# One series of 16x16 inverses on 128 partitions in place of two on 64, in a two-layer hybrid decoder step

## The chip, the cores and the metric

The kernel runs on one core of a Trainium2 chip. The metric is the device time of one execution in microseconds (us). All times in the text are of one profiled execution, in us from the start of its span, unless a sentence says otherwise. Engines: PE is TensorE (matmuls; PEld its weight loads), DVE is VectorE, ACT is ScalarE, POOL is GpSimd, and SP is SyncE, whose queue issues nearly all DMAs here.

## The reference, cut to what matters

One inference step of a decoder with two layers, on a prompt of 512 tokens and on 8 sequences of 4 sample tokens, model width 1024. A layer is a norm, one input projection (`w_in`) whose columns feed four mixers, an output projection (`w_out`), and an MLP (`w_up`, squared ReLU, `w_down`):

```python
h = rms_norm(x, prm['g_mix_pre'])
p_rw, p_s5, p_gdn, p_swa = split_cols(h @ prm['w_in'], PROJ_SPLITS)
o_rw, rw_shift, rw_S = rwkv7_mixer(p_rw, rw_shift, rw_S, prm)      # RWKV-7
o_s5, s5_re, s5_im = s5_mixer(p_s5, s5_re, s5_im, prm)             # S5
o_gdn, gdn_conv, gdn_S = gdn_mixer(p_gdn, gdn_conv, gdn_S, prm)    # gated delta rule
o_swa, swa_k, swa_v = swa_mixer(p_swa, swa_k, swa_v, start, prm['swa_sinks'])
mix = jnp.concatenate([o_rw, o_s5, o_gdn, o_swa], axis=-1) @ prm['w_out']
x = x + rms_norm(mix, prm['g_mix_post'])
f = jnp.square(jax.nn.relu(rms_norm(x, prm['g_mlp_pre']) @ prm['w_up'])) @ prm['w_down']
x = x + rms_norm(f, prm['g_mlp_post'])
```

The delta rule solves, for each chunk of 64 tokens and each head, a lower triangular system with ones on its diagonal (a 64x64 triangle A):

```python
U = lax.linalg.triangular_solve(eye + A, rhs, left_side=True, lower=True, unit_diagonal=True)
```

RWKV's recurrence, which the reference writes token by token, is computed by the kernel in chunks of 64 too, and needs the inverse of such a triangle as well.

## The kernel before

**Halves and mixers.** The tokens are worked in two halves of 256 prompt tokens; the second carries the 32 sample tokens too (288 columns). `body()` writes the work in this order: projection of half 0, mixers of half 0, `w_out` of half 0, mixers of half 1, MLP of half 0, `w_out` of half 1, and so on through the second layer; the projection of half 1 is written among the mixers of half 0. So there are four places where mixers run: place 1 (layer 0, half 0), place 2 (layer 0, half 1), place 3 (layer 1, half 0) and place 4 (layer 1, half 1).

**Order on the engines.** The program is put in order ahead of time by a scheduler that goes by priorities: `PRIO` gives a number to a named section (`gd2` 3000, `norm` 800, `rw2` 392, `rwt` 300, `gdt` 200, and so on; the section `rw3` and the matmuls of `dense` have none). Each engine, and SP's queue, then works through its own list strictly in the order written; an instruction that waits holds up all that stand behind it.

**Dense matmuls.** `dense` works unit by unit: 24 matmuls of 128x128 weights on 256 or 288 columns, in two half-units of 12. A half-unit is one 256 KB load into `wraw` (5 buffers), a cast on ACT into `whi` (3 buffers), a subtraction on DVE into `wlo` (3 buffers), and 12 matmuls (`ps<-h,whi` and `ps<-h,wlo`). The result banks of `dense` rotate over 3 buffers (bank "mm"), and the sliding-window mixer's rope, a matmul of a copied result with a permutation (`ps<-e,cst`), takes its bank from the same three. DVE frees that bank by `e<-ps,g`, which multiplies it by the rope table (a `g2` tile loaded by SP behind the delta rule's end, `last_gd`).

**The triangles.** `tri_begin` makes the inverses of the 16x16 blocks on the diagonals of a mixer's triangles: two DMAs write the triangles to DRAM (`trsc`), one gathers the diagonal blocks into a tile `c` of 64 partitions (64 blocks, one to a partition); then 23 DVE operations, each on the result of the one before (seven pairs of a product `c<-t,c` and a sum `t<-c` on 8x8 blocks, two rounds of four on the off-diagonal 8x8 blocks, one copy `t<-t`); two DMAs write the inverses and their transposes to a zeroed DRAM image (`diag`), and four read them back as block-diagonal 64x64 tiles (`t<-diag`: `t16t` and `t16`). `tri_end` then builds the whole inverses by matmuls (`ps<-t,t`) and DVE additions. `rw_stage2` (section `rw2`) and `gd_stage2` (section `gd2`) each call `tri_begin`; `gd_stage3` (`gdt`) and `rw_stage3` (`rwt`) call `tri_end`. All these tiles, and the RWKV triangles `lt` themselves, are of class `t2`, which has 5 buffers. What follows is `rw_chain` and `gd_chain` (a recurrence over four chunks), `rw_post` and `gd_post` (norm and gate; their results go to DRAM as `mix`), and `s5_main` (loads of its kernels `s5kin`, two small convolutions on PE, scans on DVE, products on POOL, 40 small matmuls for y, gelu, a round trip through DRAM `s5sz`, and a gate: the matmuls `ps<-r,r` 128x256 called GLU below). `w_out` of a half needs `mix` of all four mixers.

Of the kernel before, what the change touches and what calls it, by code (L numbers as in the profile page):

```python
# [139 lines left out]
class K:  # L140
# [133 lines left out]
    def tri_begin(self, lt, which):  # L274


        nc = self.nc
# [4 lines left out]
        for c in range(2):
            self.nc.sync.dma_start(out=rows(sc, c), in_=lt[64 * c:64 * c + 64])
        gp = self.w([64, 17, 16], "c1")
        g = gp[:, 0:16]
# [211 lines left out]
    def rw_stage2(self, l, r):  # L497
# [25 lines left out]
        tri = self.tri_begin(lt, 0)  # L523
# [26 lines left out]
        r.update(rp=rp, xv=xv, bk=bk, xw=xw, z=z, kt=kt, tri=tri)  # L550
# [330 lines left out]
    def gd_stage2(self, l, r):  # L881
# [11 lines left out]
        r.update(sco=sco, tri=self.tri_begin(sco[:, :, 1], 1))  # L893

    def gd_stage3(self, l, r):
# [22 lines left out]
        self.inv_apply(self.tri_end(*r["tri"]), kg, wt, lambda h, b, cs: vt[cs, h // 2, b, 64 * (h % 2):64 * (h % 2) + 64], xw)  # L918
# [1118 lines left out]
```

## Time and profile before

| what | value |
|---|---|
| three runs | 1645.79, 1649.16 and 1655.67 us; median 1649.16 |
| the profiled execution | 1651.66 us, its span 1649.9 us |
| PE busy / PEld busy | 1562.9 us (95%) / 1458.9 us (88%) |
| DVE busy | 1216.6 us (74%), 2959 instructions |
| ACT / POOL busy | 964.7 us (58%) / 312.8 us (19%) |
| granted TensorE clock, mean | 0.976 |

PE is busy nearly throughout, so the time is that of PE's work, plus the idle gaps in it, plus what stretches at the lower clock cost. A saving on another engine is worth what it takes out of PE's gaps. The gaps of PE over 0.5 us sum to 75.9 us; they lie at the start and end, and around the places where mixers and norms meet.

### The profile page before, as it was taken

What the parts mean: (1) busy time and instruction counts of PE and PEld (TensorE: products, weight loads), DVE (VectorE), ACT (ScalarE), POOL (GpSimd) and SP (SyncE); (2) the same over time, 40 slices, a digit from 0 to 9 for tenths busy, and PEclk for the clock granted to TensorE, in tenths of its full rate; (3) what the DMA queues carried; (4) which work ended last, traced back from release to release, by engine and by line L of the source; (5) the groups of instructions that cost most, each with busy time, mean ns of one, the idle gap of its engine ahead of it and who ended that gap; (6) DMA issues with size and microseconds to landing.
All of it is one profiled execution on the core that took longest, in us unless ns stands there. A gap on an engine that the chain in (4) does not pass through costs nothing. (4 is left out here: it accounts for less than half of the span.)

```text
span 1649.9 us, 38760 instructions
## 1 busy us (share of the span) xinstructions
PE 1562.9 (95%) x14472; PEld 1458.9 (88%) x14472; DVE 1216.6 (74%) x2959; ACT 964.7 (58%) x2094; POOL 312.8 (19%) x614
## 2 busy tenths in 40 slices
PE   6989999799999999799999999999999899999996
PEld 6878878689888999788899999989898899999996
DVE  6799785986696868778485667889668865866665
ACT  6676557654345468575465467886444456855544
POOL 4651241100112424600020002520002101100001
PEclk9999998999999999999999999999999999999998
DMA  6635443443356566435356556535534665655452
GB/s 216 197 111 129 150 148 122 118 114 122 125 192 228 191 207 231 135 96 149 117 191 190 166 160 205 184 110 147 137 119 146 226 216 188 204 193 165 161 168 104
DMA packets 205416, 267.37 MB, mean 162 GB/s; under 512 B 81114, under 2 KB 98844, under 8 KB 204812
## 3 DMA queue, kind: packets, MB, share of 16 engines
q1 hardware_dynamic: 203308, 258.73, 49.5%
q0 software_dynamic: 1920, 6.17, 1.0%
q8 instruction: 113, 1.85, 0.4%
q14 instruction: 75, 0.61, 0.1%
HBM read 237.95 MB, written 28.58 MB: 162 GB/s over the span
## 5 line engine op out<-in xcount | busy, mean ns | idle before, releaser
L232 ACT CAST whi<-wraw 128x512 fp32r<-128x512 f32 x752 | 462.8, 619 | 420.4 <-PE ps L220 244.7
L236 DVE TENSOR_TENSOR wlo<-wraw,whi 128x512 fp32r<-128x512 f32 x752 | 537.6, 721 | 215.1 <-ACT whi L232 187.2
L220 PE MATMUL ps<-h,whi 128*128 128x288 f32 (+1 forms) x3264 | 517.4, 298 | 12.7 <-ACT whi L232 6.0
L220 PEld LDWEIGHTS ps<-h,whi 128*128 128x128 f32 x3264 | 453.8, 193 | 29.3 <-ACT whi L232 7.7
L220 PE MATMUL ps<-f,whi 128*128 128x288 f32 (+1 forms) x2752 | 426.6, 294 | 5.9 <-ACT whi L232 2.8
L220 PEld LDWEIGHTS ps<-f,whi 128*128 128x128 f32 x2752 | 375.5, 191 | 17.3 <-ACT whi L232 4.3
L220 PE MATMUL ps<-h,wlo 128*128 128x288 f32 (+1 forms) x1632 | 291.9, 297 | 4.6 <-DVE wlo L236 4.3
L220 PEld LDWEIGHTS ps<-h,wlo 128*128 128x128 f32 x1632 | 238.0, 192 | 13.7 <-DVE wlo L236 7.6
L220 PE MATMUL ps<-f,wlo 128*128 128x288 f32 (+1 forms) x1376 | 236.2, 293 | 7.3 <-DVE wlo L236 7.2
L220 PEld LDWEIGHTS ps<-f,wlo 128*128 128x128 f32 x1376 | 197.3, 191 | 11.9 <-DVE wlo L236 8.7
L236 POOL TENSOR_TENSOR sums<-sums,d 128x288 f32<-128x288 f32 (+1 forms) x60 | 61.1, 1019 | 537.1 <-ACT d L228 532.9
L236 DVE TENSOR_TENSOR acc<-acc,ps 128x256 f32<-128x256 f32 (+1 forms) x96 | 41.7, 435 | 51.9 <-PE ps L220 51.7
L232 ACT CAST f<-d 128x288 fp32r<-128x288 f32 (+1 forms) x128 | 53.4, 417 | 35.7 <-DVE d L236 35.5
L220 PE MATMUL ps<-r,r 64*64 64x64 f32 (+7 forms) x1184 | 68.3, 237 | 6.3 <-DMA r<-s5m 3.1
L220 PEld LDWEIGHTS ps<-r,r 64*64 64x64 f32 (+4 forms) x1184 | 56.6, 140 | 15.5 <-issue 8.0
L228 ACT ACTIVATE d<-ps 128x256 f32<-128x256 f32 (+1 forms) x156 | 61.4, 394 | 13.3 <-PE ps L220 11.4
L228 ACT ACT_TABLE_LOAD x45 | 57.7, 1283 | 0.8
L236 DVE TENSOR_TENSOR f<-d,f 128x288 fp32r<-128x288 f32 (+1 forms) x128 | 55.4, 434 | 1.9 <-ACT f L232 1.7
L236 DVE TENSOR_TENSOR d<-d 128x288 f32<-128x288 f32 (+1 forms) x128 | 55.7, 435 | 0.3 <-ACT d L228 0.3
L232 ACT COPY e<-ps 128x256 f32<-128x256 f32 (+2 forms) x96 | 28.0, 325 | 18.1 <-PE ps L220 8.5
L220 PE MATMUL ps<-t,t 64*64 64x64 f32 x1024 | 36.5, 221 | 2.0 <-DMA t<-diag 2.0
L220 PEld LDWEIGHTS ps<-t,t 64*64 64x64 f32 x1024 | 32.6, 135 | 6.2 <-DMA t<-diag 2.4
(393 smaller groups left out, 1846.9 us busy)
## 6 DMA issues: line engine op xcount, KB each, us to landing
wraw<-in_w_up SPq DMA_DIRECT2D x256, 256.0 KB, 2.8
wraw<-in_w_down SPq DMA_DIRECT2D x256, 256.0 KB, 2.9
wraw<-in_w_in SPq DMA_DIRECT2D x176, 256.0 KB, 3.0
wraw<-in_w_out SPq DMA_DIRECT2D x64, 256.0 KB, 3.2
t<-diag SPq DMA_DIRECT2D x32, 128.0 KB, 3.2
x<-acc SPq DMA_DIRECT2D x3, 1152.0 KB, 5.3
x<-acc SPq DMA_DIRECT2D x3, 1024.0 KB, 5.1
xs<-mix SPq DMA_DIRECT2D x8, 288.0 KB, 3.3
```

Source lines behind the costliest of these rows:

```text
L220: return self.nc.tensor.matmul(out=out, lhsT=lhsT, rhs=rhs, start=start, stop=stop)
L228: return self.nc.scalar.activation(out=out, in_=in_, func=func, scale=scale, bias=bias, **kw)
L232: return self.nc.scalar.copy(out, in_)
L236: return (eng or self.nc.vector).tensor_tensor(out=out, in0=a, in1=b, op=op)
```

## The change

One `tri_begin` takes both triangles. Its tiles have 128 partitions, RWKV's 64 blocks on the lower half and the delta rule's on the upper; the 23 DVE operations and the two memsets on POOL are there once for both, after both gathers. It is called at the end of section `gd2`. The writes to `diag` are issued for the delta rule first (`for w in (1, 0)`). `t16t`, `t16` and `work` are now allocated in `tri_end`, which also issues the reads `t<-diag`. The number of DMAs stays. DVE has 92 instructions fewer (four series of 23), POOL eight.

```diff
-    def tri_begin(self, lt, which):
+    def tri_begin(self, lts):
...
-        for c in range(2):
-            self.nc.sync.dma_start(out=rows(sc, c), in_=lt[64 * c:64 * c + 64])
-        gp = self.w([64, 17, 16], "c1")
+        gp = self.w([128, 17, 16], "c1")
         g = gp[:, 0:16]
-        self.nc.sync.dma_start(out=g, in_=blocks(sc))
-        t16t, t16, work = (self.w([128, 8, 64], "t2") for _ in range(3))
...
+        half = lambda w: slice(64 * w, 64 * w + 64)
+        for w, lt in enumerate(lts):
+            sc = self.t([64 * 1040], "trsc", pool="dram", bufs=2)
+            for c in range(2):
+                self.nc.sync.dma_start(out=self.tri_rows(sc, c), in_=lt[64 * c:64 * c + 64])
+            self.nc.sync.dma_start(out=g[half(w)], in_=self.tri_blocks(sc))
+
+        tt2 = self.w([128, 2, 16, 16], "t2")
         tt = tt2[:, 0]
-        tmp = self.w([64, 16, 16], "c1")
+        tmp = self.w([128, 16, 16], "c1")
...
         nc.vector.tensor_copy(tt2[:, 1].rearrange("p j c -> p c j"), tt)
+        for w in (1, 0):
+            for x in range(2):
+                self.nc.sync.dma_start(out=self.tri_blocks(self.diag[w][x]), in_=tt2[half(w), x])
...
-        for x, t in enumerate((t16t, t16)):
-            d = self.diag[which][x]
-            self.nc.sync.dma_start(out=blocks(d), in_=tt2[:, x])
-            for c in range(2):
-                self.nc.sync.dma_start(out=t[64 * c:64 * c + 64], in_=rows(d, c))
-        return lt, t16, t16t, work
-
-    def tri_end(self, lt, t16, t16t, work):
+    def tri_end(self, lt, which):
+        t16t, t16 = (self.w([128, 8, 64], "t2") for _ in range(2))
+        for x, t in enumerate((t16t, t16)):
+            for c in range(2):
+                self.nc.sync.dma_start(out=t[64 * c:64 * c + 64], in_=self.tri_rows(self.diag[which][x], c))
+        work = self.w([128, 8, 64], "t2")
...
-        tri = self.tri_begin(lt, 0)
...
-        self.inv_apply(self.tri_end(*r["tri"]), r["kt"], r["wt"], r["z"], r["xw"])
+        self.inv_apply(self.tri_end(r["lt"], 0), r["kt"], r["wt"], r["z"], r["xw"])
...
-        r.update(sco=sco, tri=self.tri_begin(sco[:, :, 1], 1))
+        r.update(sco=sco, lt=sco[:, :, 1])
...
             self.gd_stage2(l, gd)
+            self.tri_begin((rw["lt"], gd["lt"]))
```

The scheduler gives other orders to the engines around it. Three places of place 1 are shown.

**SP, the reads of the inverses.** `diag00` and `diag01` are RWKV's, `diag10` and `diag11` the delta rule's, `wraw` the loads of half-units of `w_in`. Before:

```order
L1659 DMA wraw_547_2871<-in_w_in 128x512
L316 DMA diag00_270_1399<-t2_350_1694 64x16x16
L316 DMA diag01_271_1400<-t2_350_1694 64x16x16
L318 DMA t2_348_1692<-diag00_270_1399 64x8x64 x2
L318 DMA t2_349_1693<-diag01_271_1400 64x8x64 x2
L1659 DMA wraw_552_2903<-in_w_in 128x512
```

After, where the delta rule's inverses are read:

```order
L315 DMA diag10_272_1403<-t2_364_1784 64x16x16
L315 DMA diag00_270_1399<-t2_364_1784 64x16x16
L315 DMA diag11_273_1404<-t2_364_1784 64x16x16
L315 DMA diag01_271_1400<-t2_364_1784 64x16x16
L331 DMA t2_399_1944<-diag10_272_1403 64x8x64 x2
L331 DMA t2_400_1945<-diag11_273_1404 64x8x64 x2
```

and, 11 loads of `w_in` further on, where RWKV's are:

```order
L1670 DMA wraw_628_3354<-in_w_in 128x512
L331 DMA t2_411_2080<-diag00_270_1399 64x8x64 x2
L1670 DMA wraw_631_3372<-in_w_in 128x512
L1670 DMA wraw_636_3394<-in_w_in 128x512
L1670 DMA wraw_639_3412<-in_w_in 128x512
L331 DMA t2_412_2081<-diag01_271_1400 64x8x64 x2
```

Before, RWKV's inverses were read at once and ahead of the delta rule's (7 `w_in` loads ahead of their writes); after, they come behind the delta rule's by 11 loads for the first tile and 14 for the second. The load of the S5 kernels (`r4<-s5kin0`), which had ten `w_in` loads behind it in place 1, now stands behind the last of them.

**PE, at the 41st unit of `w_in` of half 1** (960 dense matmuls of that half done). `ps<-e1` is the rope's permutation, `ps<-r2,r4` S5's y, `ps<-g2,cst`, `ps<-r2,cst` and `ps<-acc,rwg2` belong to `gd_post` and `rw_post`, `ps441` to the end of RWKV's chain. Before:

```order
L220 MATMUL ps665_3547<-e1_664_3545,cst_6_77 128x288 [waits Activation_49]
L220 MATMUL ps666_3552<-h9_284_1440,whi_668_3554 128x288 x4
L220 MATMUL ps666_3552<-h9_285_1441,whi_668_3554 128x288 x4
L220 MATMUL ps666_3552<-h9_284_1440,wlo_669_3555 128x288 x4
L220 MATMUL ps666_3552<-h9_284_1440,whi_671_3572 128x288 x4
L220 MATMUL ps666_3552<-h9_285_1441,whi_671_3572 128x288 x3
L220 MATMUL ps478_2468<-r2_470_2445,r4_474_2461 64x64 [waits Pool_49]
```

After:

```order
L220 MATMUL ps506_2622<-g2_504_2619,cst_6_77 128x256 [waits Activation_49]
L220 MATMUL ps507_2625<-g2_504_2619,cst_6_77 128x256
L636 MATMUL ps441_2284<-r4_341_1646,r4_346_1687 64x64 x15
L220 MATMUL ps443_2315<-r2_422_2215,cst_6_77 128x256 [waits DVE_49,Activation_49]
L220 MATMUL ps444_2319<-r2_422_2215,cst_6_77 128x256 [waits PE_49]
L220 MATMUL ps446_2324<-r2_442_2314,cst_6_77 128x256 [waits DVE_49]
L220 MATMUL ps447_2327<-r2_442_2314,cst_6_77 128x256 [waits DVE_49]
L220 MATMUL ps448_2334<-r2_442_2314,cst_6_77 128x256 [waits DVE_49,Activation_49]
L220 MATMUL ps450_2340<-acc_77_406,rwg2_82_418 128x256 [waits Activation_49]
L220 MATMUL ps451_2345<-r2_442_2314,cst_6_77 128x256 [waits DVE_49,PE_49]
L220 MATMUL ps453_2351<-acc_77_406,rwg2_82_418 128x256 [waits DVE_49,PE_49]
L220 MATMUL ps664_3525<-h9_284_1440,whi_666_3527 128x288 [waits DVE_49]
```

The DVE instruction that frees `ps664`'s bank is `e1_653<-ps654,g2_643`, the rope's product; on DVE it stands here after the change:

```order
L738 COPY r2_422_2215<-ps444_2319 128x256 [waits Activation_49]
L245 SCALAR_TENSOR_TENSOR r2_442_2314<-acc_77_406,pf_4_73 128x256 [waits PE_49] x2
L236 TENSOR_TENSOR c1_449_2336<-ps448_2334,acc_77_406 128x2x64 [waits PE_49]
L236 TENSOR_TENSOR c1_449_2336<-ps448_2334,acc_77_406 128x2x64
L236 TENSOR_TENSOR r2_445_2323<-r2_422_2215,r2_445_2323 128x512 [waits DVE_49,Activation_49]
L242 TENSOR_SCALAR r2_445_2323<-r2_445_2323,pf_4_73 128x256 [waits DVE_49]
L242 TENSOR_SCALAR r2_445_2323<-r2_445_2323,pf_4_73 128x256
L236 TENSOR_TENSOR c1_452_2347<-ps451_2345,acc_77_406 128x2x64 [waits PE_49]
L236 TENSOR_TENSOR c1_452_2347<-ps451_2345,acc_77_406 128x2x64
L236 TENSOR_TENSOR e1_653_3474<-ps654_3476,g2_643_3433 128x288 [waits DMAHW4_49,Pool_49]
```

Before, RWKV's post work was done well ahead of this point (122 small matmuls more stood ahead of it), and the unit followed the permutation without a wait for DVE. After, the end of RWKV's chain and both posts stand ahead of the unit on PE, and RWKV's post stands ahead of the rope's product on DVE. `r2_445` is what the `Exp` of `rw_post` writes on ACT.

**PE, at S5's gate.** `ps483`/`ps485` before and `ps481`/`ps483` after are the GLU. Before:

```order
L220 MATMUL ps690_3674<-h9_284_1440,whi_695_3694 128x288 [waits Activation_49]
L220 MATMUL ps690_3674<-h9_284_1440,whi_695_3694 128x288 x3
L220 MATMUL ps690_3674<-h9_285_1441,whi_695_3694 128x288 x4
L220 MATMUL ps690_3674<-h9_284_1440,wlo_696_3695 128x288 [waits DVE_49]
L220 MATMUL ps690_3674<-h9_284_1440,wlo_696_3695 128x288 x3
L220 MATMUL ps483_2536<-r2_481_2533,r2_476_2465 128x256 [waits DMAHW5_49,DMAHW1_49,PE_49]
```

After:

```order
L220 MATMUL ps477_2470<-r2_457_2362,r2_473_2436 64x64 x2
L220 MATMUL ps477_2470<-r2_467_2417,r4_472_2434 64x64 x2
L220 MATMUL ps477_2470<-r2_468_2418,r4_472_2434 64x64 x2
L220 MATMUL ps708_3752<-h9_696_3688,whi_710_3754 128x256 [waits PE_49,Activation_49]
L220 MATMUL ps708_3752<-h9_696_3688,whi_710_3754 128x256
L220 MATMUL ps481_2509<-r2_479_2506,r2_474_2438 128x256 [waits DMAHW6_49,DVE_49,PE_49]
```

Before, 72 dense matmuls of `w_in` stood between the rope's permutation behind S5's y and the gate; after, all 96 dense matmuls that were left at the 41st unit stand ahead of the last of y, and two of `w_out` stand between y and the gate.

## Rows read from the trace of the kernel before

**Rows 1.** The page: busy time of the engines, share of the span, instructions.

```profile
PE 1562.9 (95%) x14472; PEld 1458.9 (88%) x14472; DVE 1216.6 (74%) x2959; ACT 964.7 (58%) x2094; POOL 312.8 (19%) x614
```

**Rows 2.** Groups of instructions on DVE: busy time, mean ns of one, idle before.

```profile
L236 DVE TENSOR_TENSOR c<-t,c 64x256 f32<-64x256 f32 (+7 forms) x72 | 21.4, 298 | 5.1 <-DMA c<-trsc 4.3
L248 DVE TENSOR_REDUCE t<-c 64x32 f32<-64x256 f32 (+7 forms) x72 | 16.8, 234 | 0.9
...
L236 DVE TENSOR_TENSOR c<-c,t 64x256 f32<-64x256 f32 x16 | 9.5, 592 | 0.1
...
L313 DVE COPY t<-t 64x256 f32<-64x256 f32 x8 | 3.0, 379 | 0.1
```

**Rows 3.** DVE's instructions on tile c: durations ns min/median/max, first and last start, forms.

```profile
L236 DVE TENSOR_TENSOR c<-ps,cst x32: 402/406/417, 407.9 to 1326.4; 64x256 f32<-64x256 f32 x16, 32x256 f32<-32x256 f32 x16
...
L236 DVE TENSOR_TENSOR c<-ps,r x16: 404/416/425, 226.5 to 1278.2; 128x256 f32<-128x256 f32 x16
```

**Rows 4.** Timeline of DVE at place 1: start, length, engine, line, operation.

```profile
127.60 0.41 DVE L248 TENSOR_REDUCE c<-c 64x32 f32<-64x256 f32 x1
...
128.85 1.41 DVE L236 TENSOR_TENSOR d<-acc,sums 128x576 f32<-128x576 f32 x2
```

**Rows 5.** Timeline of PE, same stretch; in brackets the idle time before, and what ended it.

```profile
128.48 0.71 PE L220 MATMUL ps<-f 64*128 64x128 f32 x4 [2.01 <-DVE swst L270]
130.21 3.87 PE L220 MATMUL ps<-h,whi 128*128 128x288 f32 x15 [1.03 <-ACT h L228]
```

**Rows 6.** Windows: length, busy time of each engine, granted PE clock, DMA share.

```profile
131.00:134.40 3.40, 3.40 (x16) 3.33 (x15) 3.40 (x11) 0.72 (x3) 0.00 (x0) 0.50 0.03 6
...
316.00:333.00 17.00, 9.78 (x69) 7.73 (x70) 16.04 (x46) 10.87 (x27) 0.17 (x1) 0.78 0.38 104
...
1165.25:1172.08 6.83, 6.83 (x39) 6.26 (x36) 4.50 (x13) 0.99 (x2) 0.00 (x0) 0.50 0.27 79
```

**Rows 7.** Timeline of PE, place 4.

```profile
1163.57 0.33 PE L220 MATMUL ps<-t,t 64*64 64x64 f32 x2 [2.03 <-DMA t<-diag]
```

**Rows 8.** Timeline of PE, place 1, from 228 on.

```profile
229.31 0.22 PE L220 MATMUL ps<-r,r 64*64 64x64 f32 x1
...
235.51 0.48 PE L220 MATMUL ps<-h,wlo 128*128 128x288 f32 x1
...
241.42 2.55 PE L220 MATMUL ps<-r,r 64*64 64x64 f32 x80
...
256.88 0.70 PE L220 MATMUL ps<-h,wlo 128*128 128x288 f32 x4
...
258.49 0.69 PE L220 MATMUL ps<-h,wlo 128*128 128x288 f32 x4
259.01 1.89 PE L220 MATMUL ps<-r,r 128*128 128x256 f32 x8
...
268.97 2.71 PE L220 MATMUL ps<-h,whi 128*128 128x256 f32 x11 [0.41 <-ACT h L232]
```

**Rows 9.** Timeline of ACT, RWKV's post at place 1.

```profile
205.17 0.59 ACT L232 COPY r<-ps 128x512 f32<-128x512 f32 x1 [2.87 <-PE ps L625]
...
213.59 1.28 ACT L228 ACT_TABLE_LOAD   x1
214.88 0.84 ACT L228 ACTIVATE r<-ps,cst 128x256 f32<-128x256 f32 x2
...
217.04 0.63 ACT L228 ACTIVATE r<-r 128x512 f32<-128x512 f32 x1
```

**Rows 10.** Timeline of POOL, S5 at place 1.

```profile
235.69 3.23 POOL L236 TENSOR_TENSOR r<-r 128x504 f32<-128x504 f32 x2 [4.13 <-DVE r L236]
```

**Rows 11.** Timeline of DVE, S5's gelu at place 1.

```profile
247.17 0.84 DVE L245 SCALAR_TENSOR_TENSOR r<-r,s5d,ps 128x64 f32<-128x64 f32 x4
...
251.62 0.69 DVE L245 SCALAR_TENSOR_TENSOR r<-r,r 128x512 f32<-128x512 f32 x1 [0.32 <-ACT r L228]
```

More of the change, by code (lines that the diff above doesn't have):

```diff
@@ L300, in tri_begin @@
             self.tt(tm8[:, :, 0:r, 0:r], t8[:, :, 0:r, 0:r],
-                    g8[:, :, 0:r, r].unsqueeze(2).to_broadcast([64, 2, r, r]))
+                    g8[:, :, 0:r, r].unsqueeze(2).to_broadcast([128, 2, r, r]))
             self.red(t8[:, :, 0:r, r], tm8[:, :, 0:r, 0:r], negate=True)
-        ww = self.w([64, 8, 8], "c0")
+        ww = self.w([128, 8, 8], "c0")
         t4 = tmp.rearrange("p a b -> p (a b)").rearrange("p (c i j) -> p c i j", c=4, i=8)
         for c in (0, 4):
-            self.tt(t4, tt[:, c:c + 4, 0:8].unsqueeze(2).to_broadcast([64, 4, 8, 8]),
-                    g[:, 0:8, 8:16].rearrange("p j i -> p i j").unsqueeze(1).to_broadcast([64, 4, 8, 8]))
+            self.tt(t4, tt[:, c:c + 4, 0:8].unsqueeze(2).to_broadcast([128, 4, 8, 8]),
+                    g[:, 0:8, 8:16].rearrange("p j i -> p i j").unsqueeze(1).to_broadcast([128, 4, 8, 8]))
@@ L309, in tri_begin @@
             self.red(ww[:, c:c + 4], t4)
-            self.tt(t4, ww[:, c:c + 4].unsqueeze(2).to_broadcast([64, 4, 8, 8]),
-                    tt[:, 8:16, 8:16].rearrange("p i r -> p r i").unsqueeze(1).to_broadcast([64, 4, 8, 8]))
+            self.tt(t4, ww[:, c:c + 4].unsqueeze(2).to_broadcast([128, 4, 8, 8]),
+                    tt[:, 8:16, 8:16].rearrange("p i r -> p r i").unsqueeze(1).to_broadcast([128, 4, 8, 8]))
             self.red(tt[:, c:c + 4, 8:16], t4, negate=True)
         nc.vector.tensor_copy(tt2[:, 1].rearrange("p j c -> p c j"), tt)
+        for w in (1, 0):
+            for x in range(2):
+                self.nc.sync.dma_start(out=self.tri_blocks(self.diag[w][x]), in_=tt2[half(w), x])
@@ L314, in tri_begin, with tri_blocks, tri_rows @@
+    @staticmethod
+    def tri_blocks(d):
+        return d.rearrange("(m r) -> m r", m=64)[:, :1024].rearrange("m (i t) -> m i t", t=64)[:, :, 0:16]
+    @staticmethod
+    def tri_rows(d, c):
+        return d.rearrange("(h c r) -> c h r", h=8, c=2)[c, :, :4096].rearrange("h (i t) -> i h t", t=64)
+    def tri_end(self, lt, which):
+        t16t, t16 = (self.w([128, 8, 64], "t2") for _ in range(2))
         for x, t in enumerate((t16t, t16)):
-            d = self.diag[which][x]
-            self.nc.sync.dma_start(out=blocks(d), in_=tt2[:, x])
@@ L549, in rw_stage2 @@
         self.acopy(z, zp)
-        r.update(rp=rp, xv=xv, bk=bk, xw=xw, z=z, kt=kt, tri=tri)
+        r.update(rp=rp, xv=xv, bk=bk, xw=xw, z=z, kt=kt, lt=lt)
     def rw_stage3(self, l, r):
         r["wt"] = self.w([128, 2, 2, 128], "r2")
-        self.inv_apply(self.tri_end(*r["tri"]), r["kt"], r["wt"], r["z"], r["xw"])
+        self.inv_apply(self.tri_end(r["lt"], 0), r["kt"], r["wt"], r["z"], r["xw"])
     def inv_apply(self, inv, kt, wt, z, xw):
@@ L917, in gd_stage3 @@
         xw = self.w([128, 4, 2, 64], "g2")
-        self.inv_apply(self.tri_end(*r["tri"]), kg, wt, lambda h, b, cs: vt[cs, h // 2, b, 64 * (h % 2):64 * (h % 2) + 64], xw)
+        self.inv_apply(self.tri_end(r["lt"], 1), kg, wt, lambda h, b, cs: vt[cs, h // 2, b, 64 * (h % 2):64 * (h % 2) + 64], xw)
         r.update(qg=qg, dec=dec, kd=kd, wt=wt, xw=xw)
```

4 lines of the change are left out of this document (removed).

## The prediction

> **What bounds the kernel now.** The page comes first [rows 1]: PE is busy 95% of the span, DVE 74%, ACT 58%, and 1649.9 us of span less 1562.9 us of busy PE leave 87 us of idle PE. Anything that the change takes off DVE counts only where PE waits for DVE. So the second view is the timeline of PE at the four places where mixers run, read for the bracketed idle times, and the third the windows, read for the granted clock: a stretch at 0.50 (1.2 GHz in place of 2.4) costs about half its length. The sum below is made against the profiled execution, 1651.66 us, and then carried over to the median of the runs, 1649.16 us. A difference under 0.5% (8.2 us) is about what a measurement of this kernel can't tell from none.
>
> **What is removed from DVE.** A series has nine products `c<-t,c` of 298 ns, nine sums `t<-c` of 234, two products `c<-c,t` of 592 and two sums `c<-c` of 410, and a copy of 379 [rows 2, 4]: 2.68 + 2.11 + 1.18 + 0.82 + 0.38 = 7.2 us. That the same operations cost as much on 128 partitions is taken from the nearest rows [rows 3]: a product with 256 elements from PSUM takes 402 to 417 ns on 32 and 64 partitions, and 404 to 425 on 128. The bounds are 7.2 us and, if the cost went by partitions, 14.4. I take 7.2. Four series fewer are 4 x 7.2 = 29 us less of DVE, or nothing at the other bound. The eight memsets fewer on POOL, 19% busy, lie beside PE's work and are worth nothing.
>
> The Trainium skill, page "Trainium Kernel Development and Optimization", section "Best Practices", says to always tile to 128 partitions, which speaks for the change; the row agrees that DVE's time doesn't grow with them, and by that rule alone the kernel should become faster, which is a rival below.
>
> **What of that reaches PE.** At place 1, three operations of RWKV's series stand ahead of the norm's `d<-acc,sums` at 128.85 [rows 4], and PE is idle 2.01 and 1.03 us just there, then runs 3.4 us at half clock [rows 5, 6]. After the change the one series begins behind both gathers, so behind this norm. What it gives lies between 0 and 2.01 + 1.03 + 1.7 = 4.7 us; I take 2, since the other work on DVE (6.9 of 7 us busy there) stays. At place 2 DVE is busy 16.0 of 17 us between 316 and 333 while PE is busy 9.8 [rows 6], but one series still stands in the same stretch of DVE's list, ahead of the same norm: 0 to 4 us, and I take 0.5. At place 3 there are the matmuls of an MLP beside everything: 0. At place 4 PE waits 2.03 us for `t<-diag`, and a stretch of 6.83 us at 0.50 follows [rows 6, 7], 3.4 us lost; after the change these matmuls stand later among dense ones: 0 to 5.4, and I take 3. Together a gain of 5.5 us, with 0 and 14 as ends.
>
> **What is added: a later RWKV at place 1.** The order of SP shows what moves. RWKV's inverses were read ahead of the delta rule's; now 11 to 14 `w_in` loads come between. A half-unit of 12 dense matmuls takes 1.6 us (258.49 less 256.88, [rows 8]), so with the other work between them RWKV's chain starts some 20 us behind the delta rule's and about 50 us later than before, and its end meets the 41st unit of `w_in`, `ps664`, on PE.
>
> *When PE gets there.* Before, 960 dense matmuls were done at 236.0 [rows 8]. After, 122 small ones fewer are done by then; 80 records of such, 40 matmuls, took 2.55 us [rows 8], so 122 take 7.8; with the 2 us from above, PE arrives at 226.2. The last steps of the two recurrences are left, some 3.5 us (three hops PE to DVE and back of about 1.2 each, an estimate from DVE rows of 0.4 and PE rows of 0.2 to 0.3 for their parts). So `gd_post` starts on ACT at 229.7.
>
> *What it waits for.* The bank of `ps664` is freed by the rope's product on DVE, which stands behind RWKV's `r2_445`, and so behind this row on ACT: a square 0.63, a table load 1.28, logarithms 0.84, a table load 1.28, an exponential 0.63 (for `gd_post`, at the durations of RWKV's [rows 9]), a copy 0.59, a matmul 0.5, two squares 0.8, a table load 1.28, logarithms 0.84, a table load 1.28, an exponential 0.63 [rows 9], then on DVE a product 0.69, two scalings 0.8, two products 0.5, and the rope's own 0.46: 13.0 us. The unit starts at 242.7. PE has had 4 or 5 us of the chains' and posts' matmuls in the 16.5 us since it arrived; the rest is idle.
>
> *S5 behind it.* On PE the convolutions of S5 now stand behind that unit. To the second convolution come 46 dense matmuls (6.1 us) and 2.4 us of small ones: 251.2. From the convolution's end to POOL's last product took 229.5 to 238.9, 9.4 us [rows 8, 10], and y on PE 2.55 [rows 8]: y ends at 263.2. The rest of the 96 dense matmuls ends at 258, so PE waits there too.
>
> *The open tail.* Before, y ended at 243.97, and `w_out` went on at 268.97: 25.0 us, of which 9.6 us of dense `w_in` (72 matmuls) were worked meanwhile [rows 8]. After, these stand ahead of y, and the tail lies open. Its length: the first half of the sums y + d u 0.84, from the second half to the end of gelu 247.17 to 252.31, 5.1 [rows 11]; from there through DRAM to the gate 252.31 to 259.01, 6.7; from the gate to `w_out` 9.96 [rows 8]; together 22.6, or at most 25.0. So `w_out` goes on at 285.8 in place of 268.97, 16.8 us later, the 2 us of gain already in it. Some 1.5 us more go to a slower clock after the idle stretch ahead of 242.7, by the 3.4 us at half clock that followed the idle times at 128 to 131 [rows 5, 6]. **Place 1 costs 18 us**. The ends: 6, if the table loads and the round trip of S5 lie beside each other better than in the row above; 25, if the tail takes its 25.0 and the half clock 7 us more.
>
> Places 2, 3 and 4 move RWKV back too, but there an MLP with its 32 units of `w_up` and 32 of `w_down` stands beside and behind the mixers and covers it: 0. Without that cover it would cost what place 1 does.
>
> **The sum.** 1651.66 + 18 - 3.5 (places 2 and 4; place 1's 2 us are in the 18) = 1666; the median of the runs lies 2.5 us lower than the profiled execution, so 1663.6. As likely errors of my row of waits are towards too long a row (steps counted one after the other that lie side by side), I shade it to **1661 us**, 0.7% slower.
>
> **The rivals.**
> 1. *Faster.* DVE's 29 us are paid back at PE's gaps, and RWKV's delay is hidden, because on the chip its chain ends well ahead of the 41st unit: for it speaks that PE is idle in all four places while DVE works on triangles; against it, that on PE both posts are written ahead of that unit. The gains then stand alone: 1649.2 - 5.5 to - 14, about 1640. It is decided by whether `r2_445` is done at 226. The skill's rule of 128 partitions points here.
> 2. *No difference.* The row of waits is short (place 1 costs 6 to 10), gains are 5: 1645 to 1657, about 1651.
> 3. *Much slower.* RWKV's reads stand in SP's queue ahead of weight loads and wait for `t2` buffers that the delta rule's `tri_end` must free first. If that end is late, the loads behind wait, and PE starves once the five `wraw` buffers, some 8 us of work, are used up. For it speaks that all SP's work is in order; against, that the delta rule's inverses come 11 loads earlier. From the point where it is over 8 us late each us counts: 1672 to 1680.
>
> **How the numbers follow.** The forecast (1655 to 1672) has 0.52, rival 1 0.18, rival 2 0.22, rival 3 0.08. The range to hold it 8 times in 10 reaches from 1644, leaving out most of rival 1, to 1674, leaving out most of rival 3. Faster by over 0.5% (under 1641) takes rival 1 at half its weight and a little of rival 2, 0.15; slower by over 0.5% (over 1657.4) takes the forecast but its lowest part, and rival 3: 0.55; the rest, 0.3, is no difference.
>
> **What would show it.** DVE busy falls by about 29 us, to 1188, and has 92 instructions fewer; the groups `t<-c` and `c<-t,c` have 36 with the same mean. At place 1 PE shows a gap of several us, or several small ones, ahead of a unit of `w_in`, ended by DVE's `e`; `w_out` begins at 280 or later; between S5's y and the gate PE is idle, ended by the DMA `r<-s5sz`. Places 2 to 4 keep the distances between them, but for 2 to 5 us less at place 4. I am wrong if `w_out` starts at 270 or earlier, if PE passes the 41st unit without a wait, or if the loss at place 1 comes back before place 3.

## The result, and the profile after

The changed kernel takes 1667.31 us (median of 4 runs, 1664.77 to 1672.52) where the kernel before takes 1650.32 (4 runs, 1645.79 to 1655.67): ratio 1.0107, 95% interval 1.0079 to 1.0136. It is slower by 1.1%. Its profiled execution took 1666.07 us, with a span of 1664.3, against 1651.66 and 1649.9.

The busy row of its page, against [rows 1]:

```profile
PE 1564.6 (94%) x14472; PEld 1455.6 (87%) x14472; DVE 1195.6 (72%) x2867; ACT 962.3 (58%) x2094; POOL 305.5 (18%) x606
```

DVE did lose 21 us of busy time and 92 instructions, and PE's busy time is the same to 1.7 us; of the 14.4 us by which the span grew, 12.7 are idle time of PE (1664.3 less 1564.6 is 99.7 us, before 87.0). The groups of the inverses on DVE (busy time, mean ns of one, idle before), which answer to [rows 2]:

```profile
L236 DVE TENSOR_TENSOR c<-t,c 128x256 f32<-128x256 f32 (+7 forms) x36 | 11.1, 308 | 8.4 <-issue 7.2 <-DMA c<-trsc 0.8
...
L248 DVE TENSOR_REDUCE t<-c 128x32 f32<-128x256 f32 (+7 forms) x36 | 8.6, 240 | 0.3
...
L236 DVE TENSOR_TENSOR c<-c,t 128x256 f32<-128x256 f32 x8 | 4.7, 588 | 0.0
...
L312 DVE COPY t<-t 128x256 f32<-128x256 f32 x4 | 1.5, 382 | 0.0
```

Half as many operations at the same mean (308, 240, 588 and 382 ns, where 64 partitions took 298, 234, 592 and 379): 128 partitions cost what 64 do, as the sum had it.

Where the idle time is, the timeline of PE at place 1 shows (start, length, operation, idle time before and what ended it). It answers to [rows 5, 8]:

```profile
125.14 0.71 PE L220 MATMUL ps<-f 64*128 64x128 f32 x4 [0.60 <-DVE swst L270]
126.63 1.68 PE L220 MATMUL ps<-h,whi 128*128 128x288 f32 x7 [0.78 <-ACT h L228]
...
215.85 0.79 PE L220 MATMUL ps<-h,wlo 128*128 128x288 f32 x4
...
235.99 0.67 PE L220 MATMUL ps<-acc,rwg 128*128 128x256 f32 x2 [2.38 <-DVE c L236]
236.31 0.88 PE L220 MATMUL ps<-h,whi 128*128 128x288 f32 x4
...
256.17 2.55 PE L220 MATMUL ps<-r,r 64*64 64x64 f32 x80 [0.77 <-POOL r L236]
258.64 0.51 PE L220 MATMUL ps<-h,whi 128*128 128x256 f32 x2
270.83 3.75 PE L220 MATMUL ps<-r,r 128*128 128x256 f32 x8 [11.68 <-DMA r<-s5sz]
...
281.44 1.86 PE L220 MATMUL ps<-h,whi 128*128 128x256 f32 x7 [1.06 <-ACT h L232]
```

The first two rows are the gain: the gaps ahead of and behind the norm fell from 2.01 and 1.03 us to 0.60 and 0.78. Then PE has done its 960th dense matmul at 216.6 and begins the next, the 41st unit, at 236.3. Before, the unit began at 238.6:

```profile
238.59 1.44 PE L220 MATMUL ps<-h,whi 128*128 128x288 f32 x8
```

So it begins 2.3 us earlier than before. The small matmuls of the chains and posts, which stood ahead of the 960th dense matmul, now stand behind it, and PE works on them for most of the 19.7 us. The loss lies behind this unit. S5's y ends at 258.7; two matmuls of `w_out` follow, and PE is idle for 11.68 us until S5's round trip through DRAM has landed. `w_out` goes on at 281.44, before at 268.97: 12.5 us late. There follow two windows of the changed kernel, ahead of the unit and from it to the 13th matmul of `w_out`, and behind them one of the kernel before, from the unit to the same matmul (length, busy time of PE, PEld, DVE, ACT and POOL with their instructions, granted PE clock, DMA share, GB/s):

```profile
216.64:236.31 19.67, 14.40 (x176) 10.13 (x175) 10.02 (x28) 11.86 (x20) 2.34 (x6) 0.91 0.34 99
236.31:283.31 47.00, 31.48 (x300) 26.50 (x299) 29.16 (x75) 20.58 (x50) 18.16 (x47) 0.81 0.34 111
```

```profile
238.59:270.84 32.25, 26.97 (x215) 23.34 (x213) 20.83 (x60) 19.85 (x48) 14.63 (x43) 0.84 0.48 154
```

PE is idle for 5.3 of the 19.7 us ahead of the unit. Behind it, it is idle for 15.5 us where it was for 5.3.

The rest of the program is best cut at three dense matmuls, the 1069th, 2881st and 5001st, at which both kernels have done the same work: the stretches end behind place 1, behind place 2, behind place 3, and just behind the last dense matmuls. Windows of the kernel before, in the same form:

```profile
0.00:270.84 270.84, 240.87 (x2329) 215.48 (x2329) 213.54 (x583) 167.42 (x394) 107.94 (x288) 0.96 0.50 157
270.84:620.59 349.75, 334.25 (x3325) 303.96 (x3325) 266.09 (x687) 191.68 (x414) 62.68 (x79) 0.97 0.50 159
620.59:995.08 374.49, 357.69 (x3278) 339.57 (x3277) 269.87 (x599) 222.39 (x474) 63.39 (x121) 0.99 0.51 160
995.08:1638.80 643.72, 630.06 (x5546) 599.92 (x5544) 461.08 (x1085) 381.79 (x814) 76.94 (x125) 0.99 0.52 168
```

and of the changed kernel:

```profile
0.00:283.31 283.31, 240.23 (x2328) 213.19 (x2329) 207.75 (x561) 168.09 (x396) 108.44 (x286) 0.94 0.49 150
283.31:631.62 348.31, 331.55 (x3325) 301.90 (x3325) 261.16 (x664) 189.72 (x412) 59.40 (x77) 0.97 0.52 159
631.62:1004.53 372.91, 357.50 (x3279) 338.60 (x3278) 263.48 (x576) 221.41 (x474) 59.94 (x119) 0.99 0.51 161
1004.53:1653.10 648.57, 635.31 (x5546) 601.90 (x5544) 457.20 (x1062) 381.60 (x814) 75.89 (x123) 0.99 0.52 167
```

The lengths differ by +12.5, -1.4, -1.6 and +4.9 us. At place 1 PE is idle for 13.1 us more (43.1 less 30.0), which is all of the 12.5. DVE is lighter by 5 to 6 us in each of the first three stretches (213.5 to 207.8 in the first), and places 2 and 3 are no more than 1.6 us shorter for it.

### The profile page after: what moved, and what is told of

It reads as the page before. It is cut to its first block, busy times and chain, and to the rows that moved or that the text cites. A ratio compares the mean times of both kernels' runs of the same rounds, so it can differ in the third digit from the quotient of the medians.

```text
span 1664.3 us, 38659 instructions
## 1 busy us (share of the span) xinstructions
PE 1564.6 (94%) x14472; PEld 1455.6 (87%) x14472; DVE 1195.6 (72%) x2867; ACT 962.3 (58%) x2094; POOL 305.5 (18%) x606
## 5 line engine op out<-in xcount | busy, mean ns | idle before, releaser
L232 ACT CAST whi<-wraw 128x512 fp32r<-128x512 f32 x752 | 462.3, 620 | 419.9 <-PE ps L220 281.4
L236 DVE TENSOR_TENSOR wlo<-wraw,whi 128x512 fp32r<-128x512 f32 x752 | 530.2, 711 | 225.3 <-ACT whi L232 190.1
L220 PE MATMUL ps<-h,whi 128*128 128x288 f32 (+1 forms) x3264 | 512.1, 296 | 11.1 <-ACT whi L232 3.8
L220 PEld LDWEIGHTS ps<-h,whi 128*128 128x128 f32 x3264 | 448.0, 191 | 27.4 <-ACT whi L232 5.5
L220 PE MATMUL ps<-h,wlo 128*128 128x288 f32 (+1 forms) x1632 | 285.5, 295 | 8.2 <-DVE wlo L236 8.2
L220 PE MATMUL ps<-r,r 64*64 64x64 f32 (+7 forms) x1184 | 73.6, 247 | 19.2 <-DMA r<-s5sz 12.5
L220 PEld LDWEIGHTS ps<-r,r 64*64 64x64 f32 (+4 forms) x1184 | 60.7, 149 | 30.1 <-issue 17.5
L236 DVE TENSOR_TENSOR f<-d,f 128x288 fp32r<-128x288 f32 (+1 forms) x128 | 60.5, 473 | 3.7 <-ACT f L232 3.4
L236 DVE TENSOR_TENSOR d<-d 128x288 f32<-128x288 f32 (+1 forms) x128 | 60.2, 470 | 0.2 <-ACT d L228 0.2
L245 DVE SCALAR_TENSOR_TENSOR cv<-e,pf,cv 128x256 f32<-128x256 f32 (+1 forms) x90 | 31.6, 400 | 6.0 <-POOL e L784 3.9
```

Of the source, the lines that this page charges most:

```text
L220: return self.nc.tensor.matmul(out=out, lhsT=lhsT, rhs=rhs, start=start, stop=stop)
L232: return self.nc.scalar.copy(out, in_)
L236: return (eng or self.nc.vector).tensor_tensor(out=out, in0=a, in1=b, op=op)
L245: return self.nc.vector.scalar_tensor_tensor(out=out, in0=a, scalar=s, in1=b, op0=op0, op1=op1)
```

## The experiments

**Theory.** The loss is the order: RWKV's inverses now wait for the delta rule's gather and come behind its inverses, so RWKV's chain and post end at the 41st unit, S5 comes behind them, and what S5 does after its last y on PE is no longer covered by dense matmuls. **Rivals.** The merged series costs by itself (it waits for both gathers, whatever the order); the loss is spread over the four places; DVE's time matters after all.

All comparisons are with the kernel before, run alternately on the same chip. The variants ran in groups on different chips, so two variants of different groups are compared by their ratios. The columns of places give the length of a stretch less that of before, cut as above, in one execution each. The last column is PE's idle time at place 1 and in all four stretches; before has 30.0 and 75.9 us.

The lengths of one execution are not steady. At place 1 the engines PE, DVE and ACT of e2, e8 and e11 work in exactly the order of before, and yet these stretches lie 7.4 us apart (268.6 to 276.0). Their idle times, 29.8 to 30.9 us, agree. The changed kernel itself gives +12.5 and +15.5 with idle times of 43.1 and 43.5. So a difference in length of under 7 us settles nothing by itself, and idle time is the better measure.

| kernel | median us | ratio (95%) | place 1 | place 2 | place 3 | place 4 | PE idle |
|---|---|---|---|---|---|---|---|
| changed | 1667.31 | 1.0107 (1.0079 to 1.0136) | +12.5 | -1.4 | -1.6 | +4.9 | 43.1 / 88.6 |
| changed, again (e9) | 1670.11 | 1.0121 (1.0089 to 1.0153) | +15.5 | -1.4 | 0.0 | +1.6 | 43.5 / 89.7 |
| e1 place 1 only | 1680.64 | 1.0174 (1.0126 to 1.0222) | +17.4 | +5.8 | +3.2 | +4.6 | 43.4 / 90.8 |
| e2 places 2 to 4 | 1661.62 | 1.0071 (1.0044 to 1.0097) | +5.2 | 0.0 | -2.9 | +7.6 | 30.5 / 79.2 |
| e3 RWKV first | 1659.08 | 1.0049 (1.0020 to 1.0077) | +9.2 | -4.1 | +4.2 | -2.7 | 37.9 / 86.2 |
| e4 two series, late | 1690.68 | 1.0251 (1.0200 to 1.0302) | +18.5 | +3.0 | +1.9 | +12.0 | 47.6 / 102.0 |
| e5 changed, no trip | 1674.56 | 1.0150 (1.0119 to 1.0181) | +8.0 | +6.5 | +0.5 | +7.9 | 35.0 / 86.5 |
| e6 before, no trip | 1640.50 | 0.9954 (0.9929 to 0.9980) | -7.3 | -3.0 | +6.0 | -8.1 | 28.5 / 71.5 |
| e7 before, no series | 1646.61 | 0.9975 (0.9954 to 0.9997) | +3.6 | -12.1 | +0.3 | +0.6 | 30.7 / 71.1 |
| e8 mixed | 1636.78 | 0.9919 (0.9890 to 0.9947) | -2.2 | -10.2 | -2.8 | -2.4 | 29.8 / 66.6 |
| e10 mixed, merged at 1 | 1652.25 | 1.0001 (0.9982 to 1.0021) | +9.6 | -2.5 | -0.3 | -5.0 | 36.1 / 76.3 |
| e11 place 2, RWKV first | 1644.17 | 0.9952 (0.9930 to 0.9974) | -1.0 | -9.5 | +3.2 | -5.0 | 30.9 / 73.5 |
| e12 changed, tables on DVE | 1667.16 | 1.0086 (1.0057 to 1.0115) | +16.8 | -7.9 | -0.6 | +10.2 | 41.5 / 86.0 |

**e1, e2: which place.** Both forms of `tri_begin` are kept, and a flag set at the head of `mixers` picks one:

```diff
+        self.one = (l, half) == (0, 0)     # e1; != in e2
...
+            if self.one:
+                self.tri_begin((rw["lt"], gd["lt"]))
```

> The change at place 1 alone; places 2 to 4 keep two series on 64 partitions. Theory (the loss is place 1's order: RWKV's chain ends at the 41st unit, S5's tail lies open): w_out of half 0 goes on near 281 as in the changed kernel, and the time is 11 to 13 us over before, ratio 1.006 to 1.008. Rival (the loss is in places 2 to 4 or in the merged series everywhere): 0 to 5 us over before, ratio under 1.003.

> The change at places 2 to 4 alone. Theory: place 1 is as before, and the rest is what the traces show beside it, -1.5 at place 2, -1.6 at place 3, +4.7 at place 4: 0 to 4 us over before, ratio 1.000 to 1.003. Rival (the loss is spread over the places): 8 us or more over before, ratio 1.005 or more.

Both came out slower than the theory said, and e2's 1.0071 is what the rival gave, a loss spread over the places. Place 1 alone costs 17.4 us in its stretch, and its PE idles 43.4 us there, as in the changed kernel (43.1), so the place is right. But e1 is slower than the full change, 1.0174 against 1.0107, and the theory has no term for that. Its idle time is 90.8 us against 88.6; the rest is longer busy time of PE for the same matmuls, at a lower clock: 0.967 over its profiled execution, and 0.961 to 0.974 over its runs, where the runs of before have 0.970 to 0.983. Why its clock is lower is open. e2 is 0.7% slower though its place 1 has the order of before: 5.2 us there at the same idle time, by a granted clock of 0.93 against 0.96, and 7.6 us at place 4, 2.7 of them idle time. So there is a second loss outside of place 1, which the theory does not cover. That it sits at place 4 is not shown: e1, whose place 4 is written as before, has +4.6 there.

**e3, e4: order or merging.** e3 takes RWKV first, e4 keeps two series on 64 partitions but issues both at the end of `gd2`:

```diff
-        for w in (1, 0):                     # e3
+        for w in (0, 1):
...
-        with self.section("gdt", bank="mb"):
-            self.gd_stage3(l, gd)
         with self.section("rwt", bank="ma"):
             self.rw_stage3(l, rw)
+        with self.section("gdt", bank="mb"):
+            self.gd_stage3(l, gd)
...
+        for w in (1, 0):                     # e4, in tri_begin behind both gathers
+            tt2 = self.w([64, 2, 16, 16], "t2")
...
```

> The changed kernel with RWKV's inverses written first and its whole inverse (rwt) put ahead of the delta rule's (gdt). RWKV's chain then ends at 924 dense matmuls in place of 960, and 72 dense matmuls stand between y and the gate again. Theory (the order, not the merging, is the loss): w_out of half 0 goes on within 4 us of before, and the time is at most 4 us over before, ratio 0.997 to 1.003. Rival (waiting for both gathers is the loss, whatever the order): ratio 1.007 to 1.011.

> Two series on 64 partitions as before, but both issued at the end of gd2, the delta rule's first: no DVE work is saved, and RWKV's chain ends at the 41st unit as in the changed kernel. Theory (the order costs, DVE's 29 us are worth next to nothing): 14 to 24 us over before, ratio 1.009 to 1.015. Rival (the DVE time is what counts): the saving of 29 us is lost too, and the time is 29 us or more over the changed kernel's, ratio 1.027 or more; second rival (the merged series of 128 partitions itself is slow): as before, ratio 1.000 to 1.004.

e3 lies between: half of the loss is gone, and place 1 still costs 9.2 us. RWKV's chain ends earlier than in the changed kernel (221.4, there 225.5), the 72 dense matmuls cover the tail again, but S5's products on POOL now come late for PE. PE's timeline of e3:

```profile
250.34 0.69 PE L220 MATMUL ps<-r,r 64*64 64x64 f32 x8 [5.48 <-POOL r L236]
...
268.33 1.97 PE L220 MATMUL ps<-r,r 128*128 128x256 f32 x8 [0.76 <-DMA r<-s5sz]
```

The idle time ahead of the gate fell from 11.68 us to 0.76, and 5.48 us stand ahead of y instead. So both hold: the order costs the tail, and the rest goes with waiting for both gathers, which delays RWKV in either order. In e3 the series begins on DVE at 128.2, where RWKV's began at 117.9 before, and RWKV's chain ends at 221.4, before at 205.1. e10, with the same order at place 1, has nearly the same idle time there (36.1 us, e3 37.9).

e4, with no DVE work saved and the order late, is the slowest: 1.0251. PE's timeline of e4 has both waits:

```profile
261.35 0.69 PE L220 MATMUL ps<-r,r 64*64 64x64 f32 x8 [6.88 <-POOL r L236]
...
277.06 3.75 PE L220 MATMUL ps<-r,r 128*128 128x256 f32 x8 [9.95 <-DMA r<-s5sz]
```

That is above what the theory gave. It is some 23 us over the changed kernel, where the rival by DVE's time had 29 or more (a ratio of 1.027, which lies inside e4's interval). So e4 does not rule this rival out for a late order: with RWKV's series last, DVE's 7.2 us probably do stand on the path. PE idles 4.5 us more at place 1 than in the changed kernel, and 13 us more in all. The rival by which the merged series is slow in itself falls, since e4 does without it.

**e5, e6: is the tail open.** S5's round trip through DRAM is left out, so the gate reads other numbers:

```diff
-        sz = self.t([8, 128, N], f"s5sz{half}", pool="dram", bufs=2)
...
-        zf = self.w([128, 2, 4, N], "r2")
...
+        zf = z.rearrange("p (u t) c -> p u t c", u=2)
```

> The changed kernel without S5's round trip through DRAM ahead of the gate: the gate reads gelu's result as it lies, so its numbers are others; the rest is the same. Theory (at place 1 the tail behind S5's y lies open): the idle time of 11.7 us ahead of the gate shrinks by 5 to 8 us, w_out goes on near 275, and the time is 5 to 8 us under the changed kernel's, ratio to before 1.005 to 1.008. Rival (the tail is paid elsewhere anyway, or PE's sum sets the time): ratio 1.0095 to 1.012.

> The kernel before without the same round trip. Theory (before, 72 dense matmuls cover the tail at place 1, and MLPs at the others): ratio 0.997 to 1.001. Rival (the round trip costs its 6 us in any order): ratio 0.993 to 0.996.

At place 1, e5 does what was expected. Its PE timeline:

```profile
266.33 3.75 PE L220 MATMUL ps<-r,r 128*128 128x256 f32 x8 [3.83 <-issue]
...
276.93 1.44 PE L220 MATMUL ps<-h,whi 128*128 128x256 f32 x5
```

The gap of 11.68 us is 3.83, and `w_out` goes on at 276.9 in place of 281.4; PE's idle time at place 1 is 8.1 us shorter. But the whole, 1.0150, is outside of what theory and rival gave, and not faster than the changed kernel (the intervals overlap): places 2 and 4 are 8 and 3 us longer than the changed kernel's, in an order that the scheduler made anew. e6, at 0.9954, landed in its rival's range (0.993 to 0.996), not in the theory's. Its stretch of place 1 is 7.3 us shorter, but only 1.5 of these are idle time, so the trip was not an open wait there. By idle time the pair shows the tail at place 1; it says nothing safe of the whole.

**e7: what DVE's time is worth.** The series of before without their operations, so that no inverse is computed:

```diff
-        for r in range(1, 8):
-            self.tt(tm8[:, :, 0:r, 0:r], t8[:, :, 0:r, 0:r],
...
+        nc.vector.tensor_copy(tt.rearrange("p a b -> p (a b)")[:, 1:2], g[:, 0, 1:2])
         nc.vector.tensor_copy(tt2[:, 1].rearrange("p j c -> p c j"), tt)
```

> The kernel before with the DVE operations of all eight series left out but for one small copy and the last one: the inverses are not computed, the DMAs and memsets stay. DVE has some 54 us less, twice what the change saves. Theory (DVE's time is off PE's path nearly everywhere): 0 to 8 us under before, ratio 0.995 to 1.000. Rival (DVE's time reaches PE's gaps, so that the change's saving is worth 10 us and more, hidden by the order's loss): ratio 0.990 or less.

168 operations less, some 54 us by the durations of before (DVE's busy time falls by 41.9 us, to 1174.7), and with them the longest chains to RWKV's and the delta rule's inverses, give 0.25%, 5.5 us by the medians. In proportion the change's 29 us would be worth 3 us or so; that is an estimate, and e4 shows that it does not hold in every order.

**e8, e10, e11: the order chosen by place.** Two series at place 1, one at the others, RWKV first at places 2 and 4, the delta rule first at place 3 (e8); one series at place 1 too, RWKV first (e10); one series at place 2 alone, RWKV first (e11):

```diff
+        self.one = (l, half) != (0, 0)     # e8; True in e10; (l, half) == (0, 1) in e11
+        self.rwf = half == 1               # e8; half == 1 or l == 0 in e10; True in e11
...
+        for w in ((0, 1) if self.rwf else (1, 0)):
...
+        two = [("gdt", "mb", self.gd_stage3, gd), ("rwt", "ma", self.rw_stage3, rw)]
+        for name, bank, f, x in (two[::-1] if self.rwf else two):
```

> Place 1 as before (two series), one series at places 2 to 4, RWKV's inverses first at places 2 and 4, the delta rule's first at place 3: at each place the order that was best in the traces so far. Theory (each place's order sets its own gain or loss): 0 at place 1, -4 at place 2, -2 at place 3, -3 at place 4, together -9 us, ratio 0.992 to 0.997. Rival (the differences at places 2 to 4 are chance of the clock, or change with what stands ahead): ratio 0.999 to 1.005.

> The changed kernel once more, beside the next one on one chip. Both theories: ratio 1.008 to 1.013.

> As e8, but with one series at place 1 too, RWKV's inverses first there (as in e3). Theory (merging at place 1 costs what e3's trace shows there, 9 us, because RWKV's inverses wait for the delta rule's gather; places 2 to 4 keep e8's gains): 7 to 11 us over e8, ratio 0.996 to 1.000. Rival (what stands ahead changes the later places as well, so that places can't be added up): outside of 0.994 to 1.002.

> One series at place 2 alone, RWKV's inverses first; places 1, 3 and 4 have two series. Theory (most of e8's gain is place 2's, where its trace has 10 us less, half of it clock): 5 to 11 us under before, ratio 0.993 to 0.997, and the stretch of place 2 shorter by 4 to 11. Rival (e8's gain needs all three places, or came from the clock of one execution): ratio 0.998 to 1.003.

e8 takes 1636.78 us, 0.9919 (0.9890 to 0.9947): it beats both kernels, by a hair more than was expected. Its windows, cut at the same matmuls:

```profile
0.00:268.64 268.64, 238.84 (x2328) 213.79 (x2329) 213.14 (x583) 166.68 (x394) 106.89 (x288) 0.96 0.52 159
268.64:608.23 339.59, 325.61 (x3325) 298.86 (x3325) 259.34 (x664) 191.41 (x414) 61.58 (x77) 0.98 0.53 163
608.23:979.88 371.65, 356.87 (x3279) 338.75 (x3278) 263.87 (x576) 220.84 (x474) 60.02 (x119) 0.99 0.53 161
979.88:1621.10 641.22, 633.23 (x5546) 601.14 (x5544) 455.50 (x1062) 382.00 (x814) 75.97 (x123) 0.99 0.54 169
```

Place 2's stretch is 10.2 us shorter, and e11, with one series at this place alone and the same order of instructions there as e8, is 0.9952 with 9.5 us there: over half of e8's gain is place 2's. Only 1.5 and 2.0 of these us are idle time of PE; the rest is shorter busy time for the same matmuls, at a granted clock of 0.98 against 0.97. How much of that is clock was not separated. e2 and e8 differ only in who comes first at places 2 and 4, and lie some 25 us apart (1.0071 and 0.9919); in the two traces 7.4 of these are at place 1, where their orders are the same. e10 is 0.8% over e8 (1.0001 against 0.9919, some 13 us) and just outside of what was expected (0.996 to 1.000): place 1 costs its 9.6 us again, but place 2, written as in e8, gives 2.5 in place of 10.2, and its trace shows that the scheduler has put it in another order. So gains by place add up only roughly. e9 gave the changed kernel's time again, 1.0121.

**e12: a collision at place 2.** In the changed kernel DVE's own operations are slow from 566 to 585. Its timeline of DVE, and behind it that of POOL:

```profile
571.48 1.62 DVE L236 TENSOR_TENSOR f<-d,f 128x256 fp32r<-128x256 f32 x1
573.02 1.75 DVE L236 TENSOR_TENSOR wlo<-wraw,whi 128x512 fp32r<-128x512 f32 x1
574.70 1.63 DVE L236 TENSOR_TENSOR d<-d 128x256 f32<-128x256 f32 x1
...
579.47 0.68 DVE L236 TENSOR_TENSOR wlo<-wraw,whi 128x512 fp32r<-128x512 f32 x1
...
584.82 0.68 DVE L236 TENSOR_TENSOR wlo<-wraw,whi 128x512 fp32r<-128x512 f32 x1
```

```profile
572.89 1.33 POOL L236 TENSOR_TENSOR r<-s 128x512 f32<-128x512 f32 x1
574.30 3.26 POOL L236 TENSOR_TENSOR s<-r,s5pw 128x512 f32<-128x512 f32 x2
...
579.20 0.52 POOL L1368 MEMSET r<- 128x512 f32 x1
```

`wlo` takes 1.75 us in place of 0.68 and `d<-d` 1.63 in place of 0.43 while POOL builds S5's tables for layer 1. The one `wlo` that begins while POOL is at a memset, which reads nothing, takes 0.68. The same POOL work lay at 541 to 562 before, mostly beside `w_down`. There `wlo` was as slow (1.5 to 1.9 us), but the evacuation reads PSUM (`acc<-acc,ps`, 0.41 us there throughout); now the work lies beside `w_up`, whose evacuation has two operations on SBUF to a unit, and these are slow too. The windows of these stretches, of before and then of the changed kernel:

```profile
541.00:563.00 22.00, 21.43 (x183) 20.20 (x182) 20.27 (x19) 7.84 (x13) 20.07 (x13) 1.00 0.48 158
```

```profile
566.00:585.00 19.00, 13.74 (x108) 12.72 (x106) 18.30 (x13) 6.66 (x15) 18.14 (x13) 1.00 0.34 100
```

PE loses 0.6 us of the one and 5.3 of the other. It is the same in the other traces: in e2, where the tables lie beside `w_up` too, PE is idle for 5.7 us meanwhile; in e8 and e11, where they lie mostly beside `w_down`, for 0.5 and 0.4. So part of what sets e8 apart from e2 at place 2 is where the tables fall. e12 takes the tables off POOL:

```diff
-        e = nc.vector if not l else nc.gpsimd
+        e = nc.vector
```

> The changed kernel with the 13 operations that build layer 1's S5 tables (s<-r,s5rv, s<-r,s5pw, r<-s, 128x512) on DVE in place of POOL; the scheduler may order what follows anew. Theory (while POOL works on these, DVE's operations take two to three times as long and PE loses 5.3 us of 19): without them on POOL, wlo takes 0.68 us throughout that stretch, PE's idle time there falls under 2 us, place 2's stretch gets 3 to 6 us shorter, ratio to before 1.007 to 1.010. Rival (DVE's long operations have another cause, such as the DMAs or ACT; and 13 more operations on DVE cost PE): ratio 1.011 to 1.015, PE idle as before there.

Ratio 1.0086, as the theory had it; place 2 is now at -7.9 in place of -1.4, 6.5 us shorter where 3 to 6 were expected. The window of e12 around its tables:

```profile
560.00:590.00 30.00, 30.00 (x281) 29.05 (x280) 27.02 (x49) 16.49 (x38) 0.00 (x0) 1.00 0.60 182
```

PE has no idle time in it at all, with the 13 operations on DVE, and `wlo` takes 0.68 to 0.76 us throughout, beside the same `w_up`. So the collision is shown, and at place 2 it cost PE 5 us of idle time (16.8 us in that stretch, 11.3 in e12). The gain of the whole is not shown: the interval of 1.0086 overlaps that of the changed kernel, and in this trace places 1 and 4 are longer.

## Why the prediction was right

The forecast was slower, 1661 us with 1644 to 1674; measured are 1667.31, with the loss where it was put, in the tail behind S5's y at place 1. But several terms were off, and they cancelled. Step by step:

- **DVE's saving**: 7.2 us a series and equal cost on 128 partitions were right; the four groups and `c<-c` fell by 28 us, and so did the durations of all DVE operations together. The page's busy time, which counts operations that overlap once, fell by 21 and not 29. In the groups `f<-d,f` and `d<-d` took longer by 9.6 us together, mostly by the collision above, and `wlo` 7.4 us less.
- **What reaches PE at place 1's norm**: right in kind (gaps 3.04 to 1.38 us), 2 us taken; 576 dense matmuls were done 3.8 us earlier (1.8 in e9).
- **When PE gets to the 41st unit**: mis-sized. The prediction had 226.2; it was 216.6. Between the 576th and the 960th dense matmul PE idles in neither kernel, and this stretch fell from 96.9 to 81.3 us. So the 122 small matmuls were worth 15.6 us, not 7.8; the price was taken from 40 matmuls of 64x64, and among the 122 are wider ones (128x256). The first matmul on RWKV's state came 11 us behind the delta rule's and 27 us later than before, not 20 and 50.
- **What it waits for**: right, and 2 us too short: `gd_post` began at 221.4 (forecast 229.7), the rope's product on DVE ended at 236.2, 14.9 us on (forecast 13.0). What PE does meanwhile was wrong: of 16.5 us, 4 or 5 were to be work and the rest idle; of the 19.7 measured, 14.4 are work and 5.3 idle. The longest gap, 2.38 us, is ended by RWKV's product `c` on DVE, not by `e`, and the unit begins at 236.3, where 242.7 was forecast and 238.6 was before. So the loss does not show at this unit; what stands ahead of it matters because S5 comes behind. ACT's timeline, which answers to [rows 9]:

```profile
221.36 0.63 ACT L228 ACTIVATE g<-g 128x512 f32<-128x512 f32 x1
222.01 1.28 ACT L228 ACT_TABLE_LOAD   x1
...
233.19 0.63 ACT L228 ACTIVATE r<-r 128x512 f32<-128x512 f32 x1
```

  and DVE's:

```profile
235.76 0.45 DVE L236 TENSOR_TENSOR e<-ps,g 128x288 f32<-128x288 f32 x1
```

- **The open tail**: 22.6 us forecast, 22.7 measured (258.7 to 281.4). The gap ended by `r<-s5sz` was named.
- **Place 1**: 18 us forecast, +12.5 measured (+15.5 in e9), and `w_out` went on at 281.4 in place of 285.8. PE arrived 9.6 us earlier than forecast; the last steps of the chains (4.7 us in place of 3.5), the row of waits and S5 behind it (22.4 us from the unit to the end of y, forecast 20.5) took 5 of these back. A slower clock came ahead of the unit (0.91 in the window above) and, which was not foreseen, in the tail too, behind the idle time ahead of the gate. The granted clock between y and `w_out` is 0.64, before 0.84, and the eight records of the gate take 3.75 us, before 1.89 [rows 8].
- **Places 2 to 4**: -3.5 forecast, +1.9 measured. The step that failed is place 4: the wait for `t<-diag` went (3 us taken for it), but the stretch, which was to be 2 to 5 us shorter, is 4.9 us longer in one execution of the changed kernel and 1.6 in another. Its idle time is no longer than before (13.3 and 13.7 us), so what is longer is PE's busy time for the same matmuls; what causes it was not settled. At place 2 the collision on DVE, which was not foreseen, took back 5 us. Whether places 2 to 4 would lose what place 1 does without the cover of an MLP was not tried.
- **The shading**: the sum stood at 1666 for the profiled execution, which took 1666.07, by two errors that cancel (-5.5 at place 1, +5.4 at the others): that it hit so closely is luck. The cut to 1661 was in the wrong direction.

The rival by the rule of 128 partitions (the Trainium skill, "Trainium Kernel Development and Optimization", section "Best Practices") fell for the change as it stands: the trace agrees with it on DVE, where the four groups halved, but DVE was not where the time lay (e7). With the order chosen by place, the merging at places 2 to 4 is 0.8% faster (e8). The rival of starved weight loads did not come about at place 1: up to the 960th dense matmul PE did not wait there at all behind the norm.

## What to carry to other kernels

Merging two series that came one after the other makes the first wait for the second's input: count what the delayed one has behind it (here a chain, two posts, S5 and the last of four inputs to `w_out`), not only the operations that it saves. Where a scheduler orders the program, every edit moves work all over it, so read a trace by stretches cut at points of equal work before an end-to-end time is put down to an edit, and set idle time beside length, since a stretch in the same order differed by 7 us from one execution to another here. Try the edit place by place and in both orders; here that was worth some 30 us between the change as it stands and e8. The work of an off-path engine can still collide: look what stands beside it in its new place.

## What the runs showed of the hardware

Operations of DVE with SBUF operands alone took two to four times as long while POOL read SBUF tensors (`wlo` 1.75 us for 0.68, `d<-d` 1.63 for 0.43). Those that read PSUM did not (`acc<-acc,ps`, 0.41), nor did the `wlo` that began beside POOL's memset (0.68). The Trainium skill, page "SBUF — State Buffer", section "Terms", says that DVE and GpSimd share a pair of SBUF ports which one of them holds for a whole instruction while the other is blocked; the traces agree, with 1.1 to 1.2 us more in these two rows beside POOL operations of 1.3 to 1.6. e12 shows that POOL's work is the cause; that it is the ports is the page's account, which no run here singles out.

The granted clock differs between executions of one kernel, and the time goes with it: of the 23 executions of before that ran beside e1 to e4, the fastest, at 0.982, took 1641.32 us and the slowest, at 0.970, took 1661.23. The products of the two are 1611.8 and 1611.4, so between these two the clock accounts for all of the 20 us, which is more than the change's effect. Over all 23 the times spread by 1.2% and the products by 0.7% (1605.7 to 1616.6), so the clock accounts for a good part of the spread and not for all of it.
